# A pair in seven products: the second up block split by itself, the weight sums in place and one behind the other

## The chip, the cores and the metric

The kernel runs on one core of a Trainium2 chip. The time is the device time of one execution in microseconds (us), and the median of a few runs is compared. The core has a matrix engine (TensorE, PE in the profile, with its weight loads as PEld), three engines for elementwise work (VectorE as DVE, ScalarE as ACT, GpSimd as POOL), a queue engine (SyncE, SP) that issues most loads, and 16 DMA engines that move data between DRAM and the on-chip memory. Each engine works through its own list of instructions in order and waits on semaphores for the others.

## The reference

Two residual layers over a stream of 256 tokens by 2048 features, all in float32. Layer 0 mixes with sliding-window attention and an mLSTM, layer 1 with forgetting attention, and after each mixer stands a SwiGLU feed-forward block (FFN) with 5632 hidden units:

```python
def swiglu(xn, w_gate, w_up, w_down):
    return (jax.nn.silu(xn @ w_gate) * (xn @ w_up)) @ w_down
...
    h = h + mix.astype(h.dtype)
    h = h + swiglu(rms_norm(h, norm_ffn[layer]), w_gate[layer], w_up[layer], w_down[layer])
```

A last RMS norm ends it. Nearly all the arithmetic is in products of the 256 tokens with weight matrices, and the FFN has most of them.

## The kernel before

**Precision.** A float32 product is made from three matmuls on rounded operands. A weight block `raw` (128 partitions, two rows of 512) is cast by ACT to a rounded part `hi`, and DVE subtracts to get the rest `lo = raw - hi`. `split_chunk` (lines 184 to 192) and `split_plain` (lines 356 to 358) are these two steps: the cast stands at line 188 or 357, the subtraction at 189 or 358. The activations are split once into `xh`/`xl` or `mh`/`ml`. `three` (lines 532 to 535) then does `hi·ah + lo·ah + hi·al`, 128x128 by 128x512 each, into one bank.

**Slots.** `hi` and `lo` live in eight pairs of tiles in the FFN: `slot()` hands them out in turn (names `hi`, `hi0`, `hi1` and the like). A cast into a slot waits until PE has done with what stood in it. Raw blocks have their own buffers: four for plain chunks (`wr`), five for pairs (`fp`, `RAWS`). A load is issued when the buffer it goes to has been read to its end.

**Pairs.** A group (`pair_group`) makes two neighbouring output blocks, here called gate and up (in the down projection they are two neighbouring blocks of `w_down`), from eight pairs of 128 rows; a table such as `ORDER` says which pairs are plain and which are mixed. A plain pair has eight `three` calls. A mixed pair uses a Strassen-like scheme with seven: with gate blocks `ra[0]`, `ra[1]` and up blocks `rb[0]`, `rb[1]` it needs both gate blocks, the second up block and four sums of blocks as weights, and sums of activations (`sx`, `sd`) against them. The weight sums are made by DVE at lines 606, 608 and 610:

```python
rb[:, 0, :] = ra[:, 0, :] + rb[:, 0, :]      # L606, 128x512
rb[:, 1, :] = rb[:, 0, :] - rb[:, 1, :]      # L608, 128x512
ra          = ra - rb[:, 1, :]               # L610, 128x1024, both blocks
```

(in words; the real lines are printed below). From the second part of each FFN on (`ADDING`), the first of these is done by a DMA that adds while it loads (line 600, issued by POOL). There are 103 such mixed pairs in the run, 26 of them with the sum at line 606. The branch `halves` of the same function serves the mixers and is another way to the same products.

In a mixed pair of the branch `halves is None`, before the change: ACT casts the gate blocks; DVE makes L606; ACT casts both up blocks of `rb` in one 128x1024 cast (`hu`: the sum and the raw second block); DVE subtracts; then L608 overwrites the second block, L610 the gate blocks; ACT casts the one block of `rb` (`hc`, 128x512) and then `ra` (`hd`, 128x1024), each with its subtraction behind it.

**The order.** No order is written by hand here: a planner lays each engine's list out in advance from estimated durations, and mixes work of neighbouring pairs and groups. On the chip each list is then fixed. A cast that waits for its load holds up every cast behind it on ACT.

**Stages of an FFN.** The 11 column blocks of the hidden units are cut in parts of 3, 4 and 4 (`PARTS`). Each part first makes its gate and up blocks, group by group, then the down products of that part. Between them the hidden block is transposed, the last of the first part by PE (line 693, tile `pf`) and split into `mh`/`ml`. Just before the FFN, the output projection of the mixer ends and `xh`/`xl` are split anew (line 363, tile `xl`).

Of the kernel before, what the change touches and what calls it, by code (L numbers as in the profile page):

```python
# [76 lines left out]
def trunk(  # L77
# [29 lines left out]
    def slot():  # L107
        if not stock:
            return [wp.tile([P, CK, NB], F32R, tag=a, name=a) for a in ("hi", "lo")]
        stock.append(stock.pop(0))  # L110
        return stock[-1]
# [17 lines left out]
    def load_raw(w, k0, c0, n, pool=wr, bufs=4, raws=None):  # L129
        if raws:  # L130
            raw = raws.pop(0)
            raws.append(raw)
        else:
            raw = pool.tile([P, CK, NB], F32, tag="raw", name="raw", bufs=bufs)
        loaded[0] = nc.sync.dma_start(
            raw[:, :, 0:n], w[k0 * P : (k0 + CK) * P, c0 : c0 + n].rearrange("(k p) n -> p k n", p=P)
        )
        return raw
# [42 lines left out]
    def load_chunk(w, k0, c0, n):  # L181
        raw = ahead.pop(0) if ahead else load_raw(w, k0, c0, n)
        return raw if isinstance(raw, tuple) else split_chunk(raw, n)
# [15 lines left out]
    def run_due(todo, step):  # L199
        while todo and todo[0][0] <= step:  # L200
            with tc.issue_after(latest[0].ins):
                todo.pop(0)[1]()
# [153 lines left out]
    def split_plain(dst_h, dst_l, src):  # L356
        nc.scalar.copy(dst_h, src)  # L357
        nc.vector.tensor_tensor(out=dst_l, in0=src, in1=dst_h.bitcast(F32), op=ALU.subtract)  # L358
# [173 lines left out]
    def three(o, ah, al, hi, lo, start, stop):  # L532
        nc.tensor.matmul(o, ah, hi, start=start, stop=False)  # L533
        nc.tensor.matmul(o, ah, lo, start=False, stop=False)  # L534
        nc.tensor.matmul(o, al, hi, start=False, stop=stop)  # L535

    def bank(par, name):
        return pm.tile([P, NB], F32, tag="pm", name=name) if par else pa.tile([P, NB], F32, tag="acc", name=name)

    def pair_group(fp, par, lhs, sums, mats, order, todo=(), halves=None, inner=None, raws=None, adding=False):  # L540
        plain = [[bank(par, "acc") for _ in range(NT)] for _ in range(2)]
        begun = set()

        def fresh(*at):
            known = at in begun
            begun.add(at)
            return not known

        todo = list(todo)
        prods = None  # L550
        kinds = [kind for kind, _ in order]
        t0, t1 = slice(0, P), slice(P, 2 * P)

        def combine(prods):
            c = fp.tile([P, 4, NB], F32, tag="c", name="c", bufs=1)
            nc.scalar.copy(c[:, 0, :], prods[0])
            if halves is None:
                nc.vector.tensor_tensor(out=c[:, 1, :], in0=prods[3], in1=c[:, 0, :], op=ALU.add)
                nc.vector.tensor_tensor(out=c[:, 2, :], in0=prods[2], in1=c[:, 1, :], op=ALU.add)
                nc.vector.tensor_tensor(  # L560
                    out=c[:, 1:4:2, :],
                    in0=prods[1].rearrange("p (a n) -> p a n", a=1).broadcast_to([P, 2, NB]),
                    in1=c[:, 1:3, :],
                    op=ALU.subtract,
                )
                return c
            nc.vector.tensor_tensor(out=c[:, 2, :], in0=prods[3], in1=c[:, 0, :], op=ALU.add)
            nc.vector.tensor_tensor(out=c[:, 1, :], in0=prods[2], in1=c[:, 2, :], op=ALU.add)
            nc.vector.tensor_tensor(out=c[:, 3, :], in0=prods[1], in1=c[:, 1, :], op=ALU.subtract)
            nc.vector.tensor_tensor(out=c[:, 2, :], in0=prods[1], in1=c[:, 2, :], op=ALU.subtract)  # L570
            return c

        for pos, (kind, pair) in enumerate(order):
            k0 = 2 * pair
            if inner is not None and pos == len(order) - 1:
                c = combine(prods)
                inner()
            if not kind:
                last = pos == len(order) - 1
                walk = [(i, t) for i in range(CK) for t in range(NT)]  # L580
                if last:
                    walk.sort(key=lambda it: it[1])
                for m, (w, c0) in enumerate(mats):
                    hi, lo = load_chunk(w, k0, c0, NB)
                    run_due(todo, pos)
                    for i, t in walk:
                        ah, al = lhs(k0 + i)
                        ts = slice(t * P, (t + 1) * P)
                        three(
                            plain[m][t], ah[:, ts], al[:, ts], hi[:, i, :], lo[:, i, :],  # L590
                            fresh(m, t), last and i == CK - 1,
                        )
                continue
            first, last = 1 not in kinds[:pos], 1 not in kinds[pos + 1 :]
            if first:
                prods = [bank(1 - par, "prod") for _ in range(4)]
            ra, rb = (load_raw(w, k0, c0, NB, fp, W_RAWS if halves else RAWS, raws) for w, c0 in mats)
            if adding:
                (w, c0), part = mats[0], slice(k0 * P, (k0 + 1) * P)
                nc.gpsimd.dma_start(rb[:, 0, :], w[part, c0 : c0 + NB], accum_op=ALU.add)  # L600
            hg, lg = split_chunk(ra, NB)
            run_due(todo, pos)
            hu, lu = slot()
            if halves is None:
                if not adding:
                    nc.vector.tensor_tensor(out=rb[:, 0, :], in0=ra[:, 0, :], in1=rb[:, 0, :], op=ALU.add)  # L606
                split_plain(hu, lu, rb)
                nc.vector.tensor_tensor(out=rb[:, 1, :], in0=rb[:, 0, :], in1=rb[:, 1, :], op=ALU.subtract)  # L608
                both = rb[:, 1, :].rearrange("p (a n) -> p a n", a=1).broadcast_to([P, CK, NB])
                nc.vector.tensor_tensor(out=ra, in0=ra, in1=both, op=ALU.subtract)  # L610
                hc, lc = (a[:, 0, :] for a in slot())
                split_plain(hc, lc, rb[:, 1, :])
                hd, ld = slot()
                split_plain(hd, ld, ra)
                ht = [hu[:, 0, :], hd[:, 0, :], hc, hd[:, 1, :]]
                lt = [lu[:, 0, :], ld[:, 0, :], lc, ld[:, 1, :]]
            else:
                split_plain(hu[:, 1, :], lu[:, 1, :], rb[:, 1, :])
                nc.vector.tensor_tensor(out=ra[:, 0, :], in0=rb[:, 0, :], in1=ra[:, 0, :], op=ALU.add)
                nc.vector.tensor_tensor(out=rb[:, 0, :], in0=rb[:, 1, :], in1=rb[:, 0, :], op=ALU.subtract)  # L620
                nc.vector.tensor_tensor(out=rb[:, 1, :], in0=ra[:, 0, :], in1=rb[:, 1, :], op=ALU.subtract)
                nc.vector.tensor_tensor(out=ra[:, 1, :], in0=ra[:, 1, :], in1=rb[:, 1, :], op=ALU.subtract)
                parts = []
                for src in (ra, rb):
                    hs, ls = halves.pop(0)
                    halves.append((hs, ls))
                    split_plain(hs, ls, src)
                    parts.append((hs, ls))
                where = ((0, 0), (1, 0), (1, 1), (0, 1))
                ht = [parts[a][0][:, b, :] for a, b in where]  # L630
                lt = [parts[a][1][:, b, :] for a, b in where]
            sh, sl = sums(pair)
            xa, la = lhs(k0)
            xb, lb = lhs(k0 + 1)
            three(prods[0], xa[:, t0], la[:, t0], hg[:, 0, :], lg[:, 0, :], first, last)
            three(plain[0][0], xb[:, t0], lb[:, t0], hg[:, 1, :], lg[:, 1, :], fresh(0, 0), False)
            three(plain[1][0], sh[3], sl[3], hu[:, 1, :], lu[:, 1, :], fresh(1, 0), False)
            three(prods[1], sh[0], sl[0], ht[0], lt[0], first, last)
            three(prods[2], sh[2], sl[2], ht[1], lt[1], first, last)
            three(prods[3], sh[1], sl[1], ht[2], lt[2], first, last)  # L640
            three(plain[0][1], xb[:, t1], lb[:, t1], ht[3], lt[3], fresh(0, 1), False)
        if inner is None:
            c = combine(prods)
        return plain, c
# [519 lines left out]
    with tc.tile_pool(name="od", bufs=1) as od:  # L1164
# [79 lines left out]
        for i in range(4):  # L1244
# [27 lines left out]
            def v_of(j, b, i=i, vn=vs[i]):  # L1272
# [6 lines left out]
                lambda j, b, qt=qt: qt[:, j, b * P : (b + 1) * P],  # L1279
# [107 lines left out]
```

## Time and profile before

| what | value |
|---|---|
| median of 3 runs | 2086.46 us (2084.1 to 2086.69) |
| the profiled execution's own time | 2086.12 us |
| its span, first to last instruction | 2084.4 us |
| mean granted TensorE clock | 0.996 |
| PE busy | 2066.4 us (99%), 9449 matmuls |
| DVE busy | 1804.5 us (87%) |
| ACT busy | 1383.7 us (66%) |
| DMA moved | 455.07 MB, mean 218 GB/s |

How to read it: `L534` is line 534 of the kernel. In groups of instructions, `lo<-raw,hi` names what is written and read by the program's tile names, `x648` is how often, and then come the busy time and the mean of one in ns, and the idle time of the engine just before, with what ended most of it. In the timeline the columns are start and length in us, engine, line and operation; the bracket is the idle time before it. In the windows of time, each engine has its busy time and, as x, its instructions, then the granted clock (1.00 is full), the DMA engines' busy share and GB/s. A matmul is shown with 0.39 us of length, but matmuls overlap, and their starts tell the pace.

### The profile page before, as it was taken

To read this page: it belongs to the slowest core of one execution; us is meant where nothing else is said; L and a number is where in the kernel's file an instruction comes from. 1 tells how busy PE (TensorE), PEld (TensorE's weight loads), DVE (VectorE), ACT (ScalarE), POOL (GpSimd) and SP (SyncE) were. 2 spreads that over 40 slices of the span, in tenths; PEclk is the share of its full clock that TensorE was granted. 3 is DMA by queue.
4 is the path that set the end of the run, shared out by engine and by line. 5 is a ranking of instruction groups with operands and counts; after the bars stand their busy time and mean duration, and the time that the engine had idled before them with its cause. 6 is when DMAs were issued, how large, how long until landed. Compare 5 with 4: busy or idle time off the path is not lost.

```text
span 2084.4 us, 26995 instructions
## 1 busy us (share of the span) xinstructions
PE 2066.4 (99%) x9449; PEld 1713.1 (82%) x9449; DVE 1804.5 (87%) x2235; ACT 1383.7 (66%) x1760; POOL 113.2 (5%) x143
## 2 busy tenths in 40 slices
PE   9999999999999999999999999999999999999998
PEld 7878887887888888888888888888878888888887
DVE  6788768999899998998899688679998999899994
ACT  6777677765567656767677776687655677557763
POOL 1010000000000000000010000000000000000000
PEclk9999999999999999999999999999999999999999
DMA  8566577666778777778676766587657777867864
GB/s 292 175 208 197 189 252 227 187 204 213 210 225 265 232 233 237 226 240 218 205 211 208 229 198 185 155 265 227 222 174 235 236 220 239 259 205 209 265 206 150
DMA packets 320664, 455.07 MB, mean 218 GB/s; under 512 B 107644, under 2 KB 115856, under 8 KB 320400
## 3 DMA queue, kind: packets, MB, share of 16 engines
q1 hardware_dynamic: 307088, 426.27, 64.9%
q0 software_dynamic: 12720, 25.99, 6.8%
q8 instruction: 74, 1.21, 0.2%
q10 hardware_dynamic: 720, 1.09, 0.2%
q14 instruction: 62, 0.51, 0.1%
HBM read 428.87 MB, written 2.12 MB: 207 GB/s over the span
## 4 chain that ended last, share of the span: by engine, by line
PE 86%; DMA 4%; DVE 4%; ACT 4%; issue 3%; SPq 0%; ACTq 0%; POOLq 0%; POOL 0%; DVEq 0%
PE acc L533 19%; PE acc L534 19%; PE acc L535 19%; PE prod L533 5%; PE prod L534 5%; PE prod L535 5%; PE acc L224 4%; PE acc L223 4%; PE acc L225 4%; DVE lo L189 1%; DMA raw<-in_w_down_dram 1%; ACT hi L188 1%; DMA raw<-in_w_gate_dram 1%; PE p L387 1%; ACT box L323 1%
## 5 line engine op out<-in xcount | busy, mean ns | idle before, releaser
L189 DVE TENSOR_TENSOR lo<-raw,hi 128x1024 fp32r<-128x1024 f32 (+3 forms) x648 | 762.7, 1192 | 148.5 <-ACT hi L188 146.2
L188 ACT CAST hi<-raw 128x1024 fp32r<-128x1024 f32 (+3 forms) x648 | 654.0, 1027 | 352.9 <-PE acc L535 130.1
L534 PE MATMUL acc<-lo,xh 128*128 128x512 f32 x1272 | 495.0, 390 | 0.0
L535 PE MATMUL acc<-hi,xl 128*128 128x512 f32 x1272 | 493.9, 390 | 0.0
L533 PE MATMUL acc<-hi,xh 128*128 128x512 f32 x1272 | 480.5, 391 | 2.4 <-ACT hi L188 2.4
L357 ACT CAST hi<-raw 128x1024 fp32r<-128x1024 f32 (+1 forms) x323 | 286.9, 894 | 193.7 <-DVE raw L608 78.2
L358 DVE TENSOR_TENSOR lo<-raw,hi 128x1024 fp32r<-128x1024 f32 (+1 forms) x323 | 328.3, 1026 | 31.2 <-ACT hi L357 30.4
L533 PEld LDWEIGHTS acc<-hi,xh 128*128 128x128 f32 x1272 | 239.4, 188 | 53.6 <-ACT hi L188 4.0
L534 PEld LDWEIGHTS acc<-lo,xh 128*128 128x128 f32 x1272 | 239.6, 188 | 49.7 <-issue 0.2
L535 PEld LDWEIGHTS acc<-hi,xl 128*128 128x128 f32 x1272 | 239.3, 188 | 49.9
L534 PE MATMUL acc<-lo,mh 128*128 128x512 f32 x466 | 181.4, 390 | 0.0
L535 PE MATMUL acc<-hi,ml 128*128 128x512 f32 x466 | 180.8, 389 | 0.0
L533 PE MATMUL acc<-hi,mh 128*128 128x512 f32 x466 | 176.3, 389 | 4.4 <-ACT hi L357 4.4
L610 DVE TENSOR_TENSOR raw<-raw 128x1024 f32<-128x1024 f32 x103 | 125.6, 1220 | 0.9
L224 PE MATMUL acc<-lo,mh 128*128 128x512 f32 (+1 forms) x322 | 126.3, 392 | 0.0
L223 PE MATMUL acc<-hi,mh 128*128 128x512 f32 (+1 forms) x322 | 125.8, 391 | 0.0
L225 PE MATMUL acc<-hi,ml 128*128 128x512 f32 (+1 forms) x322 | 123.7, 391 | 0.0
L533 PEld LDWEIGHTS acc<-hi,mh 128*128 128x128 f32 x466 | 87.5, 188 | 23.0 <-ACT hi L357 4.9
L534 PEld LDWEIGHTS acc<-lo,mh 128*128 128x128 f32 x466 | 87.6, 188 | 18.2
L535 PEld LDWEIGHTS acc<-hi,ml 128*128 128x128 f32 x466 | 87.6, 188 | 18.2
L224 PE MATMUL acc<-lo,xh 128*128 128x512 f32 (+3 forms) x288 | 99.9, 347 | 0.2 <-DVE lo L189 0.2
L225 PE MATMUL acc<-hi,xl 128*128 128x512 f32 (+3 forms) x288 | 98.8, 344 | 0.0
(362 smaller groups left out, 3033.1 us busy)
## 6 DMA issues: line engine op xcount, KB each, us to landing
raw<-in_w_gate_dram SPq DMA_DIRECT2D x176, 512.0 KB, 5.3
raw<-in_w_up_dram SPq DMA_DIRECT2D x176, 512.0 KB, 5.2
raw<-in_w_down_dram SPq DMA_DIRECT2D x176, 512.0 KB, 5.7
raw<-in_w_in_odd_dram SPq DMA_DIRECT2D x88, 512.0 KB, 5.1
raw<-in_w_in_even_dram SPq DMA_DIRECT2D x51, 512.0 KB, 4.7
raw<-in_w_out_even_dram SPq DMA_DIRECT2D x32, 512.0 KB, 5.1
raw<-in_w_out_odd_dram SPq DMA_DIRECT2D x32, 512.0 KB, 4.7
raw<-in_w_gate_dram POOLq DMA_DIRECT2D x56, 256.0 KB, 5.7
```

The costliest lines, as they stand in the source:

```text
L188: latest[0] = nc.scalar.copy(hi[:, k, 0:n], raw[:, k, 0:n])
L189: nc.vector.tensor_tensor(out=lo[:, k, 0:n], in0=raw[:, k, 0:n], in1=hi[:, k, 0:n].bitcast(F32), op=ALU.subtract)
L223: nc.tensor.matmul(o, ah[:, ts], hi, start=(k == 0), stop=False)
L224: nc.tensor.matmul(o, ah[:, ts], lo, start=False, stop=False)
L225: nc.tensor.matmul(o, al[:, ts], hi, start=False, stop=(k == k_all - 1 and cs.stop == n))
L323: nc.scalar.copy(ju[:, :, b], turned[:, b, :, :, :].rearrange("p k t q -> p (k t q)"))
L357: nc.scalar.copy(dst_h, src)
L358: nc.vector.tensor_tensor(out=dst_l, in0=src, in1=dst_h.bitcast(F32), op=ALU.subtract)
L533: nc.tensor.matmul(o, ah, hi, start=start, stop=False)
L534: nc.tensor.matmul(o, ah, lo, start=False, stop=False)
L535: nc.tensor.matmul(o, al, hi, start=False, stop=stop)
L610: nc.vector.tensor_tensor(out=ra, in0=ra, in1=both, op=ALU.subtract)
```

## The change

In the branch `halves is None`, the second up block is now cast and split by itself while it is still raw, into the second half of the slot `hu`. After that DVE makes the three sums in place, one behind the other, with no cast in between. Then `rb` (both blocks are sums now) and `ra` are cast and split with 128x1024 each. Which product uses which block stays as it was; only the tile that holds it differs.

```diff
             hu, lu = slot()
+            split_plain(hu[:, 1, :], lu[:, 1, :], rb[:, 1, :])
             if halves is None:
                 if not adding:
                     nc.vector.tensor_tensor(out=rb[:, 0, :], in0=ra[:, 0, :], in1=rb[:, 0, :], op=ALU.add)
-                split_plain(hu, lu, rb)
                 nc.vector.tensor_tensor(out=rb[:, 1, :], in0=rb[:, 0, :], in1=rb[:, 1, :], op=ALU.subtract)
                 both = rb[:, 1, :].rearrange("p (a n) -> p a n", a=1).broadcast_to([P, CK, NB])
                 nc.vector.tensor_tensor(out=ra, in0=ra, in1=both, op=ALU.subtract)
-                hc, lc = (a[:, 0, :] for a in slot())
-                split_plain(hc, lc, rb[:, 1, :])
-                hd, ld = slot()
-                split_plain(hd, ld, ra)
-                ht = [hu[:, 0, :], hd[:, 0, :], hc, hd[:, 1, :]]
-                lt = [lu[:, 0, :], ld[:, 0, :], lc, ld[:, 1, :]]
+                parts = []
+                for src in (rb, ra):
+                    hs, ls = slot()
+                    split_plain(hs, ls, src)
+                    parts.append((hs, ls))
+                where = ((0, 0), (1, 0), (0, 1), (1, 1))
             else:
-                split_plain(hu[:, 1, :], lu[:, 1, :], rb[:, 1, :])
...
-                ht = [parts[a][0][:, b, :] for a, b in where]
-                lt = [parts[a][1][:, b, :] for a, b in where]
+            ht = [parts[a][0][:, b, :] for a, b in where]
+            lt = [parts[a][1][:, b, :] for a, b in where]
```

The branch `halves` keeps its steps. Line 606 becomes 607 in the changed file, and lines behind 628 move up by one.

The planner lays the lists out anew. Two places matter for what follows. The first is ACT's list at the start of the first down products in layer 0 (layer 1 has the same rows with other numbers). `raw_4184` and `raw_4186` are the two loads of a mixed pair (gate and up block), `raw_4299` is a plain chunk of the next group, `mh<-pf` is the transposed hidden block. Before:

```order
L188 CAST hi0_3094<-raw_4252 128x1024
L357 CAST hi_3102<-raw_4186 128x512
L188 CAST hi_3098<-raw_4299 128x1024
L357 CAST mh_60<-pf_4062 128x512
L357 CAST hi_3104<-raw_4184 128x1024
L357 CAST mh_60<-pf_4069 128x512
```

And of the change:

```order
L188 CAST hi0_3094<-raw_4252 128x1024
L357 CAST hi_3102<-raw_4186 128x1024
L357 CAST hi_3104<-raw_4184 128x1024
L357 CAST mh_60<-pf_4062 128x512
L188 CAST hi_3098<-raw_4299 128x1024
L357 CAST mh_60<-pf_4069 128x512
```

The cast of the pair's last sums (`raw_4184`) stood behind the cast of the plain chunk and one of the `pf` casts; now it stands ahead of both.

The second is DVE's list at the start of the FFN in layer 0 (again the same in layer 1 with other numbers). `raw_3311` and `raw_3313` are a mixed pair, `raw_3494` and `raw_3496` the first of the next group, and `raw_3369` is a plain chunk whose buffer the load of `raw_3458` waits for. Before:

```order
L358 TENSOR_TENSOR lo_3109<-raw_3313,hi_3108 128x1024
L363 SCALAR_TENSOR_TENSOR xl_59<-box_3080,gT_93,xh_58 128x256 x4
L606 TENSOR_TENSOR raw_3496<-raw_3494,raw_3496 128x512
L358 TENSOR_TENSOR sx1_2411<-s4_3242,sx0_2410 128x512
L608 TENSOR_TENSOR raw_3313<-raw_3313 128x512
L189 TENSOR_TENSOR lo_3099<-raw_3369,hi_3098 128x1024
```

And of the change:

```order
L358 TENSOR_TENSOR lo_3109<-raw_3313,hi_3108 128x512
L363 SCALAR_TENSOR_TENSOR xl_59<-box_3080,gT_93,xh_58 128x256 x3
L607 TENSOR_TENSOR raw_3496<-raw_3494,raw_3496 128x512
L363 SCALAR_TENSOR_TENSOR xl_59<-box_3080,gT_93,xh_58 128x256
L608 TENSOR_TENSOR raw_3313<-raw_3313 128x512
L358 TENSOR_TENSOR sx1_2411<-s4_3242,sx0_2410 128x512
L610 TENSOR_TENSOR raw_3311<-raw_3311,raw_3313 128x1024
L189 TENSOR_TENSOR lo_3099<-raw_3369,hi_3098 128x1024
```

The sum at line 610 now stands ahead of the subtraction of the plain chunk `raw_3369`; before, it followed it. The subtraction at the head of these rows is half as long.

## The prediction

> **What bounds the kernel now.** I read the page first, then who waited for whom on PE, then the windows of time around each wait, and last the timelines of ACT, DVE and PE at those places.
>
> ```profile
> span 2084.4 us, 26995 instructions
> PE 2066.4 (99%) x9449; PEld 1713.1 (82%) x9449; DVE 1804.5 (87%) x2235; ACT 1383.7 (66%) x1760; POOL 113.2 (5%) x143
> ```
>
> PE is busy for 2066.4 of 2084.4 us. Engines beside it can't set the end on average; they count only where PE stands still. The waits of PE are few:
>
> ```profile
> PE acc L533 <- ACT hi L357: 4.4, 2, 2.4
> PE acc L533 <- ACT hi L188: 2.4, 2, 1.7
> ...
> PE prod L534 <- DVE lo L358: 0.9, 2, 0.7
> ```
>
> These three lines are 7.7 us in six waits, and all six lie in the first part of the two FFNs: at 354 and 1416 us where the gate and up groups begin (A in layer 0, C in layer 1), and at 473 and 1531 us where the first down products begin (B and D). Everywhere between them PE runs at its pace:
>
> ```profile
> 500.00:550.00 50.00, 50.00 (x222) 41.42 (x221) 43.78 (x44) 27.05 (x29) 3.42 (x4) 1.00 0.78 234
> ```
>
> 222 matmuls in 50 us are 0.225 us each. The windows at A show fewer:
>
> ```profile
> 355.00:360.00 5.00, 3.51 (x8) 2.84 (x9) 5.00 (x8) 4.50 (x6) 0.00 (x0) 0.58 0.96 336
> 360.00:365.00 5.00, 5.00 (x18) 3.94 (x17) 3.07 (x4) 0.00 (x0) 0.00 (x0) 0.74 0.98 339
> ```
>
> 26 matmuls where 44 would fit: 18 x 0.225 = 4.1 us lost. Only 1.5 us of that is idle (5.00 - 3.51); the other 2.6 us are the granted clock, which fell to 0.58 and 0.74. A wait of PE can thus cost its clock too. The same at D:
>
> ```profile
> 1528.47 0.82 PE L693 MATMUL pf<-ident,c 128*128 128x128 f32 x6
> 1531.68 0.49 PE L533 MATMUL acc<-hi,mh 128*128 128x512 f32 x1 [2.39 <-ACT hi L357]
> ...
> 1533.75 0.63 PE L535 MATMUL prod<-hi,sd 128*128 128x512 f32 x1
> 1534.18 0.63 PE L533 MATMUL prod<-hi,sd 128*128 128x512 f32 x1
> ...
> 1536.74 0.43 PE L535 MATMUL acc<-hi,ml 128*128 128x512 f32 x1
> ```
>
> Behind 2.39 us of idle the matmuls start 0.43 us apart (1533.75, 1534.18), and the last that is slow to come starts at 1536.74. Half pace over these 3.0 us, with the start before them, is some 1.7 us lost. So D costs 2.39 + 1.7 = 4.1 us.
>
> **The work itself.** The change has the same instructions of the same sizes in another order: per pair 3 casts of 128x1024 and one of 128x512, as many subtractions, and the same sums. The 128x512 one is now the raw up block. The loads are the same, and change places on SP by one or two. In the 77 pairs where a DMA adds, the cast of the second up block no longer waits for that DMA, but PE has no wait there that could go. The cost of that is nothing, on engines that are 66% and 87% busy beside a PE at 99%. Making dependent sums one behind the other could add a hand-over on DVE. The nearest row is the other branch, which does four sums in a chain:
>
> ```profile
> L621 DVE TENSOR_TENSOR raw<-raw 128x512 f32<-128x512 f32 x14 | 10.5, 750 | 0.1
> ...
> L608 DVE TENSOR_TENSOR raw<-raw 128x512 f32<-128x512 f32 x103 | 70.7, 686 | 0.9
> ```
>
> 750 against 686 ns bounds it at 0.06 us an operation, two a pair, 103 pairs: 13 us of DVE, inside its 280 us of idle time. Zero is my value for the end.
>
> What is left is where the casts and subtractions stand at A to D.
>
> **D and B: the cast behind a load.** ACT's list at D:
>
> ```profile
> 1526.16 0.62 ACT L357 CAST hi<-raw 128x512 fp32r<-128x512 f32 x1 [0.55 <-PE prod L535]
> 1529.15 1.04 ACT L188 CAST hi<-raw 128x1024 fp32r<-128x1024 f32 x1 [2.37 <-DMA raw<-in_w_down_dram]
> 1530.10 0.58 ACT L357 CAST mh<-pf 128x512 fp32r<-128x512 f32 x1
> 1530.58 1.05 ACT L357 CAST hi<-raw 128x1024 fp32r<-128x1024 f32 x1
> ```
>
> PE's 2.39 us end with the last of these, the cast of `ra`. Its data were there at 1528.26:
>
> ```profile
> 1527.04 1.22 DVE L610 TENSOR_TENSOR raw<-raw 128x1024 f32<-128x1024 f32 x1
> ```
>
> ACT stood behind a plain chunk's load for 2.37 us. In the new list the cast of `ra` stands ahead of that chunk. Step by step: cast of `rb` from 1526.16 to 1527.21 (128x1024 now); cast of `ra` at the latest from 1528.26 to 1529.31; its subtraction until 1530.5. PE leaves its transposes at 1529.29, finds both casts done, and needs the `lo` four matmuls on, at 1530.2. That leaves 0.3 us. The next chunks' casts now come due with PE 2 us earlier, and ACT has four in a row to make at 1.05 us; I put another 0.3 us there. So D pays 0.6 instead of 4.1 us if the clock stays, which it did at 2.04 us of idle (B):
>
> ```profile
> 473.11 0.49 PE L533 MATMUL acc<-hi,mh 128*128 128x512 f32 x1 [2.04 <-ACT hi L357]
> ```
>
> D gains 3.5 us, B with the same lists 2.04 - 0.6 = 1.4 us. Bounds: 4.1 and 2.0 if nothing is left over, 1.5 and 0.5 if the chunk's late load catches PE at the next product.
>
> **A and C: a release that comes later.** At A PE waits 1.72 us for the cast of a plain chunk, which waits for its load, which waited for the buffer that DVE's subtraction frees:
>
> ```profile
> 347.68 0.69 DVE L606 TENSOR_TENSOR raw<-raw 128x512 f32<-128x512 f32 x1 [0.25 <-DVE xl L363]
> ...
> 349.49 1.22 DVE L189 TENSOR_TENSOR lo<-raw,hi 128x1024 fp32r<-128x1024 f32 x1
> ...
> 352.16 1.22 DVE L610 TENSOR_TENSOR raw<-raw 128x1024 f32<-128x1024 f32 x1
> ```
>
> ```profile
> 355.40 1.04 ACT L188 CAST hi<-raw 128x1024 fp32r<-128x1024 f32 x1 [3.27 <-DMA raw<-in_w_gate_dram]
> ```
>
> ```profile
> 356.49 0.80 PE L533 MATMUL acc<-hi,xh 128*128 128x512 f32 x1 [1.72 <-ACT hi L188]
> ```
>
> In the new list L610 stands ahead of that subtraction (349.49), and its 1.22 us come first. Two things come off: the 0.25 us of idle ahead of L606, as another operation fills it, and 0.53 us since the subtraction a few rows up is 128x512 (0.69 against 1.22 us). So the load goes out 0.4 to 1.2 us later; I take 0.7, nearer to the end at which everything fits. PE has two more matmuls ahead of the waiting one (products of the sums moved forward), 0.45 us of work. Net +0.3 us at A (0 to 0.8). At C the lists are the same and the end of the wait is a load as well:
>
> ```profile
> 1417.68 0.50 PE L533 MATMUL acc<-hi,xh 128*128 128x512 f32 x1 [0.64 <-ACT hi L188]
> ```
>
> so +0.3 there too. C's idle time goes to about 0.9 + 0.7 = 1.6 us (the load's delay counts in full, and the two matmuls are done before it), under B's 2.04, so its clock should stay. The two short waits on `lo L358` (0.9 us together) stand just ahead of these; without them PE only comes sooner to the load.
>
> **All other pairs.** The sums reach PE later within a pair: the first by L608 (0.69 us), at most by L608 and L610 (1.9 us). Cover is PE's lead. In the first part, away from A:
>
> ```profile
> 378.24 0.69 DVE L358 TENSOR_TENSOR lo<-raw,hi 128x512 fp32r<-128x512 f32 x1
> ```
>
> ```profile
> 384.21 0.39 PE L534 MATMUL prod<-lo,sx 128*128 128x512 f32 x1
> ```
>
> The part made at 378.93 is read at 384.21: 5.3 us of lead against 1.9. Cost 0.
>
> **Sum.** -3.5 - 1.4 + 0.3 + 0.3 = -4.3 us. The profiled execution took 2086.12 us (1.72 around its span), 0.34 under the median; 2086.12 - 4.3 = 2081.8, and on the median 2086.46 - 4.3 = 2082.2 us.
>
> **The rivals.**
>
> 1. C loses its clock as A did, since its idle time grows. For: A and D closed at 2.4 us of idle. Against: B did not at 2.04, and C comes to 1.6. Price 1.7 us (D) to 2.6 us (A), in the middle 2.1: the sum is -2.2, 2084.3.
> 2. A and C don't come later, because the work that moved up meets loads that land in time, and A keeps its clock: -4.9 - 2.6 = -7.5, or 2079.0; with A's clock lost as now -4.9, 2081.6. For: L606's wait is short. Against: L610 is in front in the list whatever lands.
> 3. Slower: the longer chain of sums eats PE's lead in the 26 pairs that also make L606 on DVE, where DVE has the most to do (87% over the whole run). It decides where the lead falls under 1.9 us. With 0.4 us a pair that is 10.4 us: 2086.46 - 4.3 + 10.4 = 2092.6. Against: the 5.3 us above, and no wait in these stages now.
> 4. The gain moves on: the loads of `w_down` at B and D set the pace, so what ACT no longer holds up waits a product later for the plain chunk. Then B and D give 0.5 and 1.5, the sum is -1.4: 2085.1. For: ACT's 2.37 us are a load. Against: in the new list the first matmul on that chunk stands 18 matmuls (4 us) behind the pair's.
> 5. D's 1.7 us of slow clock are not there in most runs, so that they can't be won: the sum is -1.8 - 1.4 + 0.6 = -2.6, 2083.9. For: the three runs of before lie 2.6 us apart (2084.1 to 2086.69), about one such loss. Against: two of the three and the profiled one lie together at the upper end.
>
> The Trainium skill ("TensorE: Matmul & The Clock Gate", section Part 1) says that the clock halves after at least one idle window of about 3.4 us, and that this window runs freely. By the first no wait here would close it, and the sum would be rival 5's; the trace disagrees, as it closed behind 2.39 us at D. By the second D's loss would come and go between runs, which one profile can't show.
>
> **Chances.** The forecast 0.42 (its own range 2080.5 to 2084.5), rival 1 0.13, rival 2 0.14, rival 3 0.12, rival 4 0.12, rival 5 0.07. A difference below 0.2% (4.2 us) can't be told from none. The forecast lies at that edge, a little over half of it beyond (0.23); with rival 2 (0.13) and strays from the others (0.05) faster has 0.41. Slower is most of rival 3 and something that I don't see in the new lists: 0.14. The rest is 0.45. The range goes from 2078.5 (just under rival 2 with the clock kept) to 2088 (rivals 1 and 4 together, -1.4 + 2.1, with A and C at their upper bound, +1.0: 2088.2). Rival 3 is left out.
>
> **What would show it.** Right: no wait of PE on `hi L357` of 2 us around 473 and 1531 us, full granted clock there, ACT's cast of `ra` ahead of the wait for `w_down`. At A and C a wait on `hi L188`, a few tenths longer, with the load as its end. Wrong: waits on `lo L358` or `hi L357` of products inside a part, or a granted clock under 0.9 at C, or PE idle over 12 us in all.

## The result: slower by 0.4%, with the forecast sum at A to D and a loss elsewhere

| kernel | median of 5 runs | range |
|---|---|---|
| before | 2086.69 us | 2084.1 to 2089.03 |
| changed | 2095.78 us | 2093.21 to 2098.92 |

The ratio is 1.0041, with a 95% interval from 1.0028 to 1.0054. The forecast was 2082.2 us, and the measured time lies above its range (2078.5 to 2088.0).

The page of the changed kernel, and PE's waits in it (us in total, times, longest):

```profile
PE 2068.4 (99%) x9449; PEld 1712.1 (82%) x9449; DVE 1802.6 (86%) x2235; ACT 1379.2 (66%) x1760; POOL 110.6 (5%) x143
```

```profile
PE prod L534 <- DVE lo L358: 8.0, 4, 2.2
PE acc L533 <- ACT hi L188: 4.6, 3, 3.1
...
PE acc L223 <- DVE h L371: 1.2, 1, 1.2
```

The engines do the same work as before. The waits on `hi L357` (4.4 us, B and D) are gone. A new one heads the list: four waits on `lo L358`, 8.0 us together. PE's timeline has them at these places:

```profile
661.38 0.50 PE L534 MATMUL prod<-lo,sx 128*128 128x512 f32 x1 [1.91 <-DVE lo L358]
...
912.90 0.50 PE L534 MATMUL prod<-lo,sx 128*128 128x512 f32 x1 [2.09 <-DVE lo L358]
...
1727.39 0.50 PE L534 MATMUL prod<-lo,sx 128*128 128x512 f32 x1 [2.23 <-DVE lo L358]
...
1976.98 0.50 PE L534 MATMUL prod<-lo,sx 128*128 128x512 f32 x1 [1.75 <-DVE lo L358]
```

Twice in each FFN, in the last gate and up group of parts 2 and 3: places at which PE did not wait before. They lie in the stages with the adding DMA, where the prediction had put a cost of nothing.

**Where the time went.** Windows of 50 us hold 222 matmuls at full pace. The windows of A, B, C and D, of before and then of the changed kernel:

```profile
350.00:400.00 50.00, 47.59 (x196) 38.53 (x195) 45.59 (x56) 33.37 (x37) 0.00 (x0) 0.93 0.64 202
450.00:500.00 50.00, 47.96 (x215) 39.33 (x215) 48.55 (x56) 26.08 (x31) 0.95 (x1) 1.00 0.61 193
1400.00:1450.00 50.00, 49.15 (x216) 40.04 (x215) 49.47 (x64) 38.38 (x47) 0.00 (x0) 1.00 0.64 202
1500.00:1550.00 50.00, 47.61 (x206) 38.58 (x205) 48.21 (x56) 26.92 (x33) 0.00 (x0) 0.97 0.62 197
```

```profile
350.00:400.00 50.00, 46.89 (x200) 38.01 (x199) 46.78 (x56) 34.33 (x39) 0.00 (x0) 0.97 0.72 215
450.00:500.00 50.00, 49.17 (x219) 39.73 (x218) 47.85 (x53) 27.72 (x31) 0.95 (x1) 1.00 0.61 182
1400.00:1450.00 50.00, 48.62 (x215) 39.95 (x214) 45.47 (x63) 38.05 (x50) 0.00 (x0) 1.00 0.66 202
1500.00:1550.00 50.00, 49.02 (x218) 39.64 (x217) 47.21 (x56) 29.25 (x35) 0.00 (x0) 1.00 0.72 235
```

At 0.225 us each, 4 more matmuls at A are -0.9 us, 4 more at B -0.9, one less at C +0.2, 12 more at D -2.7: together -4.3 us, the sum of the forecast. The windows of the four new waits hold 222 matmuls each in the kernel before, and in the changed kernel:

```profile
650.00:700.00 50.00, 48.09 (x205) 39.32 (x204) 45.70 (x54) 31.31 (x36) 3.47 (x4) 0.97 0.77 223
...
900.00:950.00 50.00, 47.91 (x212) 39.34 (x210) 46.76 (x55) 31.49 (x36) 3.44 (x4) 1.00 0.79 230
...
1700.00:1750.00 50.00, 47.77 (x211) 39.03 (x210) 47.90 (x56) 32.24 (x37) 3.40 (x4) 1.00 0.80 242
...
1950.00:2000.00 50.00, 48.25 (x213) 39.63 (x212) 47.70 (x56) 32.42 (x38) 3.42 (x4) 1.00 0.82 245
```

With the window from 600 us (218 instead of 222) 51 matmuls or 11.5 us are lost around the four new waits, and about 1.0 us more at the end of layer 0 (the wait on L371, 1.19 us where it was 0.18). That makes -4.3 + 12.5 = 8.2 us of the 9.1 measured.

**What stands in DVE's way at 913 us.** The timeline of DVE in the changed kernel:

```profile
906.45 0.68 DVE L608 TENSOR_TENSOR raw<-raw 128x512 f32<-128x512 f32 x1
907.05 0.74 DVE L678 SCALAR_TENSOR_TENSOR c<-c,r 128x512 f32<-128x512 f32 x1
909.88 0.69 DVE L608 TENSOR_TENSOR raw<-raw 128x512 f32<-128x512 f32 x1 [2.09 <-DMA raw<-in_w_gate_dram]
910.49 1.22 DVE L610 TENSOR_TENSOR raw<-raw 128x1024 f32<-128x1024 f32 x1
911.62 2.35 DVE L358 TENSOR_TENSOR lo<-raw,hi 128x1024 fp32r<-128x1024 f32 x2
```

DVE is idle for 2.09 us, and the idle time ends with an adding load. PE's wait is as long, 2.09 us, and ends with the subtraction at 911.62. DVE's list tells why the two hang together (`raw_7350` and `raw_7352` are the pair in hand, `raw_7420` is the up block of the next pair):

```
L608 TENSOR_TENSOR raw_7352<-raw_7352 128x512
L678 SCALAR_TENSOR_TENSOR c_7221<-c_7221,r_3113 128x512
L608 TENSOR_TENSOR raw_7420<-raw_7420 128x512
L610 TENSOR_TENSOR raw_7350<-raw_7350,raw_7352 128x1024
L358 TENSOR_TENSOR lo_3099<-raw_7352,hi_3098 128x1024
```

The first sum of the next pair stands ahead of the last sum and the subtraction of the pair in hand. It waits for the next pair's adding load, and what PE needs is queued behind it. In the whole list an L608 of an adding pair stands ahead of the pair before's L610 exactly four times, and these are the four waits. In the list of before it never does: L608 had to come behind the cast of `hu`, so ACT waited for the adding load.

**The load is late as well.** POOL's issue of this load, as windows from the start up to it (x after PE's busy time counts matmuls). Before, the last one of part 2 and of part 3 in layer 0:

```profile
0.00:650.19 650.19, 643.51 (x3018) 530.33 (x3019) 546.45 (x748) 440.01 (x619) 35.18 (x61) 0.99 0.71 218
0.00:898.19 898.19, 891.51 (x4112) 735.68 (x4113) 776.06 (x998) 598.99 (x792) 52.47 (x81) 1.00 0.73 223
```

The same loads in the changed kernel:

```profile
0.00:651.63 651.63, 645.94 (x3029) 531.74 (x3030) 546.00 (x748) 440.30 (x620) 35.15 (x61) 1.00 0.71 218
0.00:903.00 903.00, 895.41 (x4121) 737.80 (x4122) 775.21 (x998) 597.49 (x793) 52.45 (x82) 1.00 0.73 221
```

They go out 11 and 9 matmuls later in PE's work, 2.5 and 2.0 us. The code fits that: the up buffer is now freed by a subtraction of 128x1024 behind the sums, where it was one of 128x512. So there are two candidates: the place of L608 in DVE's list, or the lateness of the load.

### The profile page after: what moved, and what is told of

It reads as the page before. It is cut to its first block, busy times and chain, and to the rows that moved or that the text cites. A ratio compares the mean times of both kernels' runs of the same rounds, so it can differ in the third digit from the quotient of the medians.

```text
span 2094.0 us, 27074 instructions
## 1 busy us (share of the span) xinstructions
PE 2068.4 (99%) x9449; PEld 1712.1 (82%) x9449; DVE 1802.6 (86%) x2235; ACT 1379.2 (66%) x1760; POOL 110.6 (5%) x143
## 4 chain that ended last, share of the span: by engine, by line
PE 67%; DVE 13%; DMA 8%; issue 6%; ACT 5%; SPq 0%; ACTq 0%; POOL 0%; DVEq 0%; POOLq 0%
PE acc L534 15%; PE acc L535 14%; PE acc L533 14%; DVE lo L189 4%; PE acc L223 4%; PE acc L224 4%; PE acc L225 4%; DMA raw<-in_w_gate_dram 3%; PE prod L534 3%; PE prod L535 3%; PE prod L533 3%; DVE lo L358 3%; ACT hi L188 2%; DMA raw<-in_w_up_dram 2%; DVE raw L608 1%
## 5 line engine op out<-in xcount | busy, mean ns | idle before, releaser
L357 ACT CAST hi<-raw 128x1024 fp32r<-128x1024 f32 (+1 forms) x323 | 286.2, 893 | 219.8 <-PE acc L535 73.5
L358 DVE TENSOR_TENSOR lo<-raw,hi 128x1024 fp32r<-128x1024 f32 (+1 forms) x323 | 327.7, 1024 | 29.1 <-ACT hi L357 28.6
L610 DVE TENSOR_TENSOR raw<-raw 128x1024 f32<-128x1024 f32 x103 | 125.5, 1219 | 1.1
```

## The experiments

Times are medians, ratios are to the kernel before on the same chip.

### 1 and 2: one half of the change at a time

```diff
+            old = halves is None and adding        # experiment 2: not adding
+            if not old:
                 split_plain(hu[:, 1, :], lu[:, 1, :], rb[:, 1, :])
...
+                if old:
+                    split_plain(hu, lu, rb)
```

with the steps of before or of the change behind it. The lists are then, in each part of the FFN, exactly those of one kernel or the other.

> The new order stays in the 26 pairs whose first sum DVE makes; the 77 pairs in which a DMA adds go back to the order of before. The lists are then those of the changed kernel in the first part of each FFN and those of before in the other two. Theory (the four new waits come from the adding pairs alone, terms A to D from the first part alone): the waits at 661, 913, 1727 and 1977 us are gone, A to D keep their -4.3 us, so 2086.5 - 4.3 = 2082 us, ratio to before 0.998. Rival (the longer chain of sums costs time in the 26 pairs, rival 3 of the prediction): the loss of 9 us stays, about 2095 us, ratio 1.0045.

> The reverse: the new order in the 77 pairs in which a DMA adds, the order of before in the 26 others. Theory: the four new waits are all there and the gain at A to D is not, so 9.3 + 4.3 = 13 to 14 us over before, about 2100 us, ratio 1.0065. Rival (chain of sums in the 26 pairs): as before, 2086 us, ratio 1.000.

Experiment 1: 2080.88 us, ratio 0.9968 (0.9955 to 0.998). Experiment 2: 2096.93 us, 1.0043 (1.0029 to 1.0057). PE's waits of experiment 1 and of experiment 2:

```profile
PE acc L533 <- ACT hi L188: 3.3, 2, 2.2
```

```profile
PE prod L534 <- DVE lo L358: 7.3, 7, 1.7
PE acc L533 <- ACT hi L357: 4.3, 2, 2.2
```

The loss sits in the adding pairs and the gain in the other 26; rival 3's pairs lose nothing. The gain is larger than expected: 15, 5 and 9 matmuls more at A, B and D and 2 fewer at C are 6.1 us, all that was measured. A gave most of the difference, as its clock stayed at 1.00. That is luck in part: the lists at A are the changed kernel's, which makes 200 matmuls in that window where experiment 1 makes 211. Experiment 2's loss is 4 us smaller than expected. Its four waits are 0.9 to 1.7 us, and its clock stayed full in the window from 650 us.

### 3: the place in the list alone

```diff
+                with tc.issue_after(behind[-1].ins) if behind and adding else ExitStack():
                     nc.vector.tensor_tensor(out=rb[:, 1, :], in0=rb[:, 0, :], in1=rb[:, 1, :], op=ALU.subtract)
...
+                behind.append(nc.vector.tensor_tensor(out=ra, in0=ra, in1=both, op=ALU.subtract))
```

> The changed kernel, with one edge for the planner: in an adding pair, L608 is not put ahead of the L610 of the pair before it in DVE's list. That moves L608 at the four places of the new waits and little else. The loads, the order of steps in a pair and the late release of the up buffer stay. Theory 'place in the list' (L608 of the next pair waits on DVE for its adding load, with the subtractions that PE needs queued behind it): the four waits are gone, L608 has no idle time of 2 us ahead of it that counts, 2086.5 - 4.3 = 2082 us, ratio 0.998. Rival 'late load' (the up buffer is freed later, so the adding load lands some 2 us later, and whoever needs it waits wherever it stands): the waits move a few matmuls on and stay near 2 us each, 2092 to 2096 us, ratio 1.003 to 1.0045.

2085.73 us, ratio 0.9995 (0.9986 to 1.0004). The windows up to the same two loads, and DVE and PE behind the second (L608, L610 and L678 are lines 611, 613 and 681 here):

```profile
0.00:649.91 649.91, 644.94 (x3028) 531.24 (x3029) 545.86 (x748) 440.14 (x620) 35.27 (x62) 1.00 0.70 218
0.00:898.31 898.31, 893.18 (x4120) 736.19 (x4121) 774.78 (x997) 597.04 (x793) 52.55 (x81) 1.00 0.72 222
```

```profile
902.12 0.68 DVE L611 TENSOR_TENSOR raw<-raw 128x512 f32<-128x512 f32 x1
902.73 0.74 DVE L681 SCALAR_TENSOR_TENSOR c<-c,r 128x512 f32<-128x512 f32 x1
903.39 1.21 DVE L613 TENSOR_TENSOR raw<-raw 128x1024 f32<-128x1024 f32 x1
904.53 0.68 DVE L611 TENSOR_TENSOR raw<-raw 128x512 f32<-128x512 f32 x1
905.13 1.21 DVE L358 TENSOR_TENSOR lo<-raw,hi 128x1024 fp32r<-128x1024 f32 x1
```

```profile
906.40 0.50 PE L534 MATMUL prod<-lo,sx 128*128 128x512 f32 x1 [0.17 <-DVE lo L358]
```

The load is as late as in the changed kernel (matmuls 3028 and 4120). L610's 1.2 us now stand ahead of the next L608, the load has landed by 904.53, and DVE doesn't stand still. All four waits shrink to 0.2 us. So the place of L608 made them, with the load as it was: from a ratio of 1.0041 to 0.9995, some 9.6 us. That the place alone would have made them isn't shown. DVE stood still for 1.7 to 2.1 us at the four places, and at the two shown above the load went out 2.0 to 2.5 us late; by these numbers little would be left of the waits with a load on time.

Against experiment 1 (0.9968) 0.27% is left, about 5.6 us (7.7 us between the two profiled executions). Three pieces are seen. At A the clock fell here and not in experiment 1: 205 matmuls in the window from 350 us against 211, or 1.4 us, with the same lists. PE waits 2.17 us on L371 at 1016 us, where experiment 1 waits 0.26. And the windows from 650, 900, 1700 and 1950 us have 220, 220, 218 and 219 matmuls against 222, 222, 223 and 223: 13 matmuls or 2.9 us at the places of the four waits. L608 still waits 1.9 to 2.7 us for an adding load at four other places, at 628, 876, 1689 and 1938 us; nothing that PE lacks at once stands behind it there, and PE shows no wait over 0.2 us.

### 4 and 5: no adding DMA

```diff
-ADDING = 3
+ADDING = 99
```

in the changed kernel (4) and in the one before (5).

> The changed kernel with the first sum made by DVE in all 103 pairs and no adding DMA at all (ADDING = 99). L608 of the next pair still stands ahead of L610 of the pair before at the same four places, but there is no adding load to wait for; DVE gets 77 sums of 0.69 us more, 53 us of its 291 us of idle time. Theory (the stall is the adding load's landing): no wait of 2 us at L608 for a load of w_gate; the plain load of the up block alone is awaited by L607, 6 us earlier in its chain, so at most 0.5 us at each place; total 2082 to 2088 us, and below the changed kernel. Rival (the chain of sums one behind the other is itself too long for PE's lead in the late parts): the four waits stay and grow by the 0.69 us of the added sum, 2098 us or more, ratio 1.006 or more.

> The kernel before with the first sum made by DVE in all 103 pairs and no adding DMA (ADDING = 99): the control for the changed kernel without adding DMA, which took 2099.75 us. There the four waits of 2 us were gone, but many of 0.2 to 0.9 us stood in their place. Theory (the changed kernel lost to the adding load; without one the new order is no worse): the same 4 us above the changed kernel's counterpart, 2100 to 2104 us. Rival (the new order costs time in the late parts whether or not a DMA adds): 2088 to 2093 us, below the counterpart.

Experiment 4: 2099.75 us, 1.0061 (1.0047 to 1.0074). Experiment 5: 2121.66 us, 1.0164 (1.015 to 1.0178). The waits of 4 and then of 5:

```profile
PE acc L534 <- DVE lo L189: 2.7, 7, 0.5
PE prod L534 <- DVE lo L358: 2.6, 4, 0.9
```

```profile
PE acc L534 <- DVE lo L189: 6.2, 15, 1.3
PE prod L533 <- DVE c L675: 4.7, 4, 1.2
```

Against the kernel before, both expectations for 4 were off in part: the time is near what the rival asked for, and the waits are not. L608 stands ahead of L610 at the same four places, but with no load to wait for it has no idle time, and no wait on `lo L358` is over 0.9 us. The control tells what the time means. Without the adding DMA the kernel before loses 35 us to the 77 sums, and the new order wins 22 us back. My 4 us for that were far too few. The new order is no loss in the late parts as such; it is one together with the adding DMA.

### 6, 7 and 8: how late may the buffer be freed?

Experiment 6 is the kernel before with the second split of an adding pair taking both blocks. Experiment 8 is experiment 1 with a copy of one column that keeps the buffer busy behind the pair's last subtraction:

```diff
-                hc, lc = (a[:, 0, :] for a in slot())       # 6
-                split_plain(hc, lc, rb[:, 1, :])
+                hr, lr = slot()
+                if adding:
+                    split_plain(hr, lr, rb)
...
+                    with tc.issue_after(split.ins):         # 8
+                        nc.vector.tensor_copy(hold, rb[:, 0, 0:1])
```

> The kernel before, but in the 77 adding pairs the second cast and subtraction of rb take both blocks (128x1024) as in the changed kernel; half of it is not used. So the up buffer comes free as late in its chain as in the changed kernel, and DVE gets 77 x 0.53 = 41 us more work, while L608 stays behind the cast of the sum, as before. Theory 'place in the list': no wait of 2 us for the pair's subtraction at the last gate and up groups of parts 2 and 3; 2086 to 2090 us, ratio 1.000 to 1.0015. Rival 'late load': waits of about 2 us at those four places, 2094 us or more, ratio 1.0035 or more.

> The kernel with the old order in adding pairs (2080.9 us), with one copy of a single column (128x1) of the up block more per adding pair, held behind the pair's last subtraction in DVE's list. It costs DVE 77 x about 0.07 us, under 6 us, and keeps the up buffer busy until there, in the list one to three subtractions of 1.2 us later than before; so its next load, and the adding load behind that, go out some 1 to 4 us later. The kernel with the second split of both blocks did that too, but gave DVE 41 us more work besides, and took 58 us longer. Theory 'late load by itself costs little where nothing else queues behind it': 2081 to 2086 us, ratio 0.997 to 1.000, no wait of PE over 1.5 us in the late parts. Rival 'the late load alone made the waits': 4 waits or more of about 2 us in the late parts, 2092 us or more, ratio 1.003 or more.

Experiment 6: 2145.05 us, 1.0279 (1.0259 to 1.03). Experiment 8: 2140.9 us, 1.0268 (1.0254 to 1.0282). Both are misses by more than 50 us. By the rivals' own words lateness would have been proven, but the price is far over theirs too, and neither run changes lateness alone.

Experiment 6 also gives DVE 41 us more work, in stages in which DVE has little room (the view from 590 us below). In experiment 8 the copies take 147 ns each, 11.3 us in all on DVE, and the time grows by 60 us, but not all of that is the copies' doing. The window from 400 us, in which PE waits in neither kernel and no copy runs yet (the first is at 523 us), in experiment 1 and then in experiment 8:

```profile
400.00:450.00 50.00, 50.00 (x222) 41.41 (x221) 46.78 (x56) 31.86 (x37) 0.00 (x0) 1.00 0.65 211
```

```profile
400.00:450.00 50.00, 50.00 (x219) 40.72 (x218) 45.98 (x56) 30.96 (x36) 0.00 (x0) 1.00 0.68 217
```

With the full clock the matmuls start 0.230 us apart where they started 0.227 us apart. Of the 58.7 us between the two profiled executions some 27 come little by little, mostly in this way, and no run shows why; the edit also adds a tile, which moves other tiles in the on-chip memory, and that wasn't tested by itself. The other 32 us are lost at four places: 186, 184, 184 and 180 matmuls in the 50 us from 640, 890, 1720 and 1980 us, where experiment 1 has 222. These are the last gate and up groups of parts 2 and 3 again, now with L608 in its old place. The chain of waits at the second of them has two adding loads, with only a cast (1.06 us) and a subtraction (1.22 us) between them (start, length):

```profile
887.22 8.42 DMA raw<-in_w_gate_dram
...
897.96 6.18 DMA raw<-in_w_gate_dram
```

Waits for `w_gate` hold ACT's casts (L358 here) up 12 times, 37.1 us in all. In experiment 6 ACT waited for adding loads 24 times, 84.2 us. So a late adding load is dear at these places. How much of the price is lateness by itself isn't shown: the planner laid out the lists around these places anew in both runs, by more than the edit. That the lead is short could be read in the kernel before, in the view of line 600:

```profile
who waited for it (us, times):
  ACT hi L357: 6.4, 4
```

ACT already waits for the adding load in 4 pairs of 77 (at 622, 870, 1682 and 1930 us, about 40 us ahead of the places of the four new waits): the lead is used up there. And DVE, with 87% over the whole run, is at 93% (400.16 of 430 us) in parts 2 and 3 of layer 0:

```profile
590.00:1020.00 430.00, 429.82 (x1919) 356.43 (x1918) 400.16 (x450) 283.75 (x329) 28.36 (x33) 1.00 0.78 227
```

Experiment 7 asked where the rest of experiment 3 lies: the new order with the edge in gate and up groups, the old order in adding pairs of the down products.

```diff
-            old = halves is None and adding
+            old = halves is None and adding and lhs is not x_of
```

> The changed kernel with L608 held behind the L610 of the pair before (2085.7 us) still lies 4.9 us over the kernel with the old order in adding pairs (2080.9 us). Here the adding pairs of the down products go back to the old order, those of the gate and up groups keep the new one, with the edge. If the rest lies in the down products (their trace shows 2.2 us of wait at the end of layer 0, PE for L371, which the old order hasn't): about 2081 to 2082.5 us, ratio 0.997 to 0.998. If it lies in the gate and up groups: 2084 to 2086 us, ratio 0.999 to 1.000.

2087.36 us, ratio 1.0003 (0.9994 to 1.0012). That is no gain over experiment 3, so the down products alone don't hold the rest. It is not a clean answer: the window from 950 us now has 211 matmuls where experiments 1 and 3 have 227 and 225, so the seam between the two orders has a loss of its own, and A has only 199 in the window from 350 us, with the clock at 0.97. What experiment 3 still loses in the late parts, 2.9 us at the four places and some 2 us at L371, stays open. That the loads are 2 us later fits it, but no run shows it. The opposite test, a sixth raw buffer so that loads go out earlier, is not among the runs.

## Why the prediction was wrong

**Terms A to D.** Their sum was -4.3 us, and the windows show -4.3. That the sums agree is luck: A came out 1.2 us better than forecast, B and D together 1.3 us worse. D was -3.5 and came to -2.7: the 2.39 us of wait and the lost clock are gone, but three waits of 0.3 to 0.4 us are left where 0.6 us were allowed. B was -1.4 and came to -0.9. C was +0.3 and came to +0.2; its wait is 1.4 us where 1.6 were expected, with full clock, so rival 1 fell. At A the wait is longer (3.1 against 1.7 us, the load as its end) but the clock lost less, and the sum is -0.9 where I had +0.3; with the same lists experiments 1, 3 and 7 have 211, 205 and 199 matmuls there, against 200 in the changed kernel and 196 before, so one profile doesn't fix this term. Experiment 1, with these four terms alone, took 2080.88 us, inside the forecast's own range.

**"All other pairs ... Cost 0".** This is the step that failed, with some 12 us, together with what "The work itself" says of the adding pairs. Three points were wrong:

1. The lead of 5.3 us was read at 378 and 384 us, in the first part, where no load adds. It says nothing of the 77 pairs of the other stages.
2. "The loads are the same, and change places on SP by one or two." They are the same, but the adding loads go out 2.0 to 2.5 us later, as the buffer is freed later. A lead of an adding load was not looked at; four pairs of before had none.
3. "The cast of the second up block no longer waits for that DMA, but PE has no wait there that could go." The wait does not go away, it moves: from ACT's cast, with nothing urgent behind it, to L608 on DVE, with the next subtractions for PE behind it. The list showed the four places before any run. The prediction named what is queued behind a waiting instruction for ACT at D, and not for DVE here.

Rival 3 had the right sign and, at 2092.6 us, about the right time, but for another cause. It put the loss into the 26 pairs that make L606 on DVE. Experiment 1 leaves these pairs in the new order and is the fastest of all. The new waits are no slow sums either: DVE stood still for 2 us.

The range left out rival 3 as the one case on the slow side. With the adding load unread, that side had too little weight.

**A better version.** Experiment 1 beats both kernels: 2080.88 us, 0.32% under before (0.20% to 0.45%).

## What to carry to other kernels

When an edit removes a dependency on a load from one instruction, look for the next instruction that has it, on which engine it stands and what is queued behind it there: a wait that is harmless on one engine can cost its whole length on another. Read the lead of a stage in that stage, loads included, and read who already waits for them: an engine at 87% over the run had 93% where it mattered. And where two parts of an edit act on different stages, keep it only in the stage in which it pays.

## What the runs showed of the hardware

**The clock.** PE's wait of 1.91 us at 661 us cost the clock (0.70 in the 5 us from 660). The waits of 2.09 us at 913 and 2.23 us at 1727 didn't (1.00 in the 10 us around each), nor did 2.20 us at A in experiment 1; 3.11 us at A in the changed kernel did. So the length of the wait doesn't decide at around 2 us. What does is how much of it falls into one window of a fixed raster. In the ten traces each spell of half clock between the start and the end of the run lasts 3.41 us or twice that, and within a run the spells start whole multiples of 3.413 us apart. The changed kernel in windows of this raster, at 661 and at 913 us:

```profile
658.62:662.03 3.41, 1.50 (x7) 0.94 (x6) 3.41 (x4) 3.28 (x5) 0.00 (x0) 1.00 0.41 83
662.03:665.45 3.42, 3.42 (x10) 2.65 (x9) 3.42 (x4) 3.42 (x5) 0.00 (x0) 0.50 0.54 88
...
911.21:914.62 3.41, 1.72 (x7) 1.42 (x8) 3.41 (x4) 3.41 (x5) 0.00 (x0) 1.00 0.49 100
914.62:918.04 3.42, 3.42 (x17) 2.81 (x15) 3.42 (x4) 3.42 (x4) 0.00 (x0) 1.00 0.78 98
```

At 661 us all 1.91 us of the wait lie in one window, and the next window runs at half clock. At 913 us the wait lies in two windows, 0.40 and 1.69 us, and the clock stays. Over all ten traces (the first 40 and the last 15 us left out) every window at full clock with 2.0 us or more of idle PE was followed by one at half clock (13 of 13), none with less than 1.5 us was, and in between it went either way (11 of 19). B's 2.04 us in the kernel before kept the clock since they lay as 0.79 and 1.25 us, so the prediction's measure for C, its length against B's, was not the one that counts. The Trainium skill ("TensorE: Matmul & The Clock Gate", section Part 1) says that the window over which activity is judged is about 3.4 us long and runs freely; these rows agree with both. The Trainium skill also says there that the clock halves after at least one idle window. That such a window has to be idle from end to end these rows don't bear out: 1.91 of 3.41 us were enough.

**Late by little, slow by much.** I had not expected a copy of 0.147 us per pair, placed so that it frees a buffer later, to come with 60 us over 77 pairs. About half of that is the slower pace of the matmuls in experiment 8, 0.230 against 0.227 us, with no shown cause. The other half falls at four places. In the chain shown there an adding load took 8.42 us, the cast and the subtraction behind it 2.3 us, and the next adding load 6.18 us; that lateness by itself makes PE pay there is argued from this chain and not shown by a run that changes nothing else.
